# Attention's small products at new places in the projection's fill, and the mLSTM's splits ordered behind attention's exponentials

## The chip, the cores and the metric

The kernel runs on one core of one Trainium2 chip. The metric is the time on the device in microseconds (us), the median of several runs. A core has five engines that run on their own and wait for one another by semaphores: TensorE (PE in the profile; PEld is its weight load), VectorE (DVE), ScalarE (ACT), GpSimd (POOL) and SyncE (SP, which here only issues DMAs). Each engine takes its instructions in the order in which the program has them: an instruction that waits holds up all that stand behind it on its engine.

## What is computed

Two layers of a decoder trunk on 512 tokens of width 1024, in float32. Cut to what matters:

```python
h = rmsnorm(x, norm_mix)
z = h @ w_in          # attention q, k, v | mLSTM q, k, v, o-gate, i/f | branch gates A, B
att = sliding_window_attention(q_a, k_a, v_a, sinks)   # 8 heads of 64, 2 key heads, window 128
hm  = mlstm_chunkwise(q_m, k_m, v_m, i_pre, f_pre)     # 4 heads
hm  = rmsnorm(hm, head_gain) * sigmoid(o_m)
x = x + (sigmoid(g_a) * (att @ w_att_branch) + sigmoid(g_m) * (hm @ w_m_branch)) @ w_out
u = relu(rmsnorm(x, norm_ffn) @ w_ff1)
x = x + (u * u) @ w_ff2
```

Attention's queries and keys go through an RMS norm for each head and a rotation of the first 16 of 64 dimensions. Scores are masked to a band, and a learned sink for each head joins the softmax's sum.

## The kernel before

**Two stages for each layer.** `mixer` does all up to `w_out`, `mlp` the rest. The change lies in `mixer` alone, and it runs twice, once for each layer.

**Large products.** A float32 product is made of three products of halves: each operand x is split into a rounded high part (ACT, a copy to fp32r) and the rest (DVE, a subtraction). `chunk` loads 128 rows of weights and splits them so (L192 on ACT, L193 on DVE); `mm3` issues the three products (L47). The large products write "mm" tiles in PSUM, the small ones "aux" tiles. There are six "mm" banks, and only two "aux" buffers, shared by all small products.

**Fill and side.** `weave(fill, side)` sets the order in which the work is written down. The fill is a list of steps of large products, each with a width: one step is 0.25, three products of 512 columns. Four steps (one chunk of weights against four column blocks) are one unit, twelve products. The side is a list of pairs (place, function): a function is called when the fill has reached its place. Tile's planner then makes each engine's order out of it: what was written earlier has the higher rank among what the planner's own model holds to be ready, so an engine's order can depart from the lists.

**The two fills of the mixer.** The first holds attention's query projection (places 0 to 8) and its key/value projection, 264 columns wide (8 to 16). The second starts with the mLSTM's query/key projection (0 to 8), then gate groups 0 and 1 (8 to 16, 16 to 24), the mLSTM's values (24 to 32), attention's two branch products `a_steps` (32 to 40), gate group 2, the o-gate and gate group 3 (40 to 64). Beside the second fill run attention (places 0 to 23 in the lists before), the mLSTM's gating (8.45 to 17.45) and, from place 28 on, the mLSTM's decay, weights and outputs.

**Attention by units.** A unit is a block b of 128 queries and a key head kv, eight in all. Each has five steps: `att_scores` for two pairs of heads (PE; ACT copies the previous block's part, L653; DVE the masked own part, L654), `att_softmax` (DVE takes the maximum, L665 to L668; ACT the exponentials, L671 and L673; DVE the sum and the scaling, L674 to L676), `att_probs` (PE transposes, `split` on ACT and DVE, L204 and L205, masks on POOL), and `att_out` (PE against the values; ACT and DVE join and split the result, L704 to L712). Ahead of them, `k_tr` and `q_tr(b)` turn keys and queries: four transposes on PE, then pairs of ACT (L632) and DVE (L633), the next pair after the last. `q_vec` and `k_vec` scale and rotate them on DVE and POOL (the keys' last step is L598). `last_exp` holds the last exponential of the softmax that was written down last.

**The row of inverse norms.** The token norm is not applied to the input but to the projections. `norm.columns` makes it as a column for each block of tokens (L270 to L276; L276 is also the last step of the head norms' inverse roots), `norm.along` as a row: four DVE writes of a diagonal (L329), one product with ones on PE, one ACT copy (L333). The row is used by the evacuations of the mLSTM's query/key projection (L724, L726) and of the gate groups (L761).

**The mLSTM's splits.** `qk_split` makes the high and low parts of the mLSTM's queries and keys, eight calls at places 12.5 + 1.4 n: ACT copies (L732), for the queries POOL copies them and DVE subtracts (L734, L737), for the keys DVE alone subtracts (L740). Their first readers are the mLSTM's weights, from place 29.75 on.

**The sigmoids.** At place 24.5 the eight tiles of gate groups 0 and 1 go through ACT's sigmoid (L748) behind `last_exp[0]`, and `back` reloads the exponential's table behind them (L754).

An instruction inside `with tc.issue_after(i)` is put behind instruction i in the order of its engine, without a semaphore.

Of the kernel before, what the change touches and what calls it, by code (L numbers as in the profile page):

```python
# [12 lines left out]
AF = mybir.ActivationFunctionType  # L13
# [5 lines left out]
NB = T // P  # L19
# [16 lines left out]
def hybrid_kernel(ctx, tc, x, norm_mix, w_in, att_q_norm, att_k_norm, att_sinks, m_gate_bias,  # L36
# [3 lines left out]
    ve, sc, gp = nc.vector, nc.scalar, nc.gpsimd  # L40
# [299 lines left out]
    norm = norm0 = Norm(lambda k: g_mix(0, k))  # L340
# [89 lines left out]
    def mixer(l, norm, late, order, phase):  # L430
# [24 lines left out]
        row = []  # L455
# [4 lines left out]
        def ev_kv(b, ps):  # L460
# [2 lines left out]
        weave(tok_steps(acts, wcols(C_Q, 512), ev_q, order=order)  # L463
              + tok_steps(acts, lambda k: [W[k * P:(k + 1) * P, C_K:C_K + 256],
                                           W[k * P:(k + 1) * P, C_IF:C_IF + 8]], ev_kv, width=264),
              late + [(6.9, norm.columns)])


        ig = sm([P, NB, MH], "ig", 1)
# [113 lines left out]
        last_exp = []  # L583
# [31 lines left out]
        def q_vec(b):  # L615
            rope(q_tok[b].rearrange("p (h d) -> p h d", d=HD), b, HQ)

        def q_tr(b):


            ps = aux()
            for j in range(4):
                pe.transpose(ps[:, j * P:(j + 1) * P], q_tok[b][:, j * P:(j + 1) * P], ident)
            for j in range(2):
                qT[b, j] = temp(F32R)
                t4 = qT[b, j].rearrange("p (n i t) -> p n i t", n=2, i=2)
                p4 = ps[:, 2 * j * P:2 * (j + 1) * P].rearrange("p (n t) -> p n t", n=2)
                for i in range(2):
                    r = slice(64 * i, 64 * i + 64)
                    o = slice(64 - 64 * i, 128 - 64 * i)  # L630
                    g = gcols[0][r, l:l + 1]
                    sc.activation(t4[r, :, i, :], p4[r], AF.Copy, scale=g)  # L632
                    ve.scalar_tensor_tensor(t4[o, :, i, :], p4[r], g, f32(t4[r, :, i, :]), op0=ALU.mult,  # L633
                                            op1=ALU.subtract)

        def att_scores(b, kv, hp):
            if hp == 0 and b:
                sps[b, kv] = temp()
            ps = aux()
            for i in range(2):  # L640
                c = 2 * hp + i
                lhs = qT[b, kv][:, c * P:(c + 1) * P]
                o = ps[:, i * 2 * P:(i + 1) * 2 * P]
                ks = slice(b * P, (b + 2) * P)
                if b == 0:

                    o, ks = o[:, P:], slice(P, 2 * P)
                pe.matmul(o, lhs, kTh[:, kv, ks], start=True, stop=False)
                pe.matmul(o, lhs, kTl[:, kv, ks], start=False, stop=True)
            p4 = ps.rearrange("p (h w k) -> p h w k", h=2, w=2)  # L650
            dst = sps[b, kv][:, hp * 2 * P:(hp + 1) * 2 * P].rearrange("p (h k) -> p h k", h=2)
            if b:
                sc.activation(dst, p4[:, :, 0, :], AF.Copy)  # L653
            ve.copy_predicated(dst, tri_i.unsqueeze(1).to_broadcast([P, 2, P]), p4[:, :, 1, :])  # L654
# [5 lines left out]
        def att_softmax(b, kv):  # L660
            sp = sps[b, kv]
            s3 = sp.rearrange("p (h k) -> p h k", h=4)
            hs = slice(4 * kv, 4 * kv + 4)
            m = sm([P, 4], "m")
            ve.tensor_reduce(m, s3, axis=AX.X, op=ALU.max)  # L665
            ve.scalar_tensor_tensor(m, m, -1.0, nsinks[:, l, hs], op0=ALU.mult, op1=ALU.min)
            es = sm([P, 4], "es")
            ve.tensor_tensor(es, sinks[:, l, hs], m, op=ALU.add)  # L668
            den = sm([P, 4], "den")
            for i in range(4):  # L670
                sc.activation(s3[:, i, :], s3[:, i, :], AF.Exp, bias=m[:, i:i + 1],  # L671
                              accum_out=den[:, i:i + 1])
            last_exp[:] = [sc.activation(es, es, AF.Exp)]  # L673
            ve.tensor_tensor(den, den, es, op=ALU.add)  # L674
            ve.reciprocal(den, den)
            ve.tensor_tensor(s3, s3, den.unsqueeze(2).to_broadcast([P, 4, P]), op=ALU.mult)  # L676

        def att_probs(b, kv):
            sp = sps[b, kv]
            pt = aux()  # L680
            for i in range(4):
                pe.transpose(pt[:, i * P:(i + 1) * P], sp[:, i * P:(i + 1) * P], ident)
            hl = split(pt, get=lambda: temp(F32R))
            parts[b, kv] = [(hl, b)]
            if b > 0:

                prev = [temp(F32R) for _ in hl]
                for src, dst in zip(hl, prev):
                    s3, d3 = (t.rearrange("p (h q) -> p h q", h=4) for t in (src, dst))
                    gp.affine_select(out=d3, in_=s3, compare_op=ALU.is_gt, fill=0.0, base=0,  # L690
                                     pattern=[[0, 4], [-1, P]], channel_multiplier=1)
                    gp.affine_select(out=s3, in_=s3, compare_op=ALU.is_ge, fill=0.0, base=0,
                                     pattern=[[0, 4], [1, P]], channel_multiplier=-1)
                parts[b, kv].append((prev, b - 1))

        def att_out(b, kv):
            po = aux()
            ls = parts[b, kv]
            for n, (pr, kb) in enumerate(ls):
                vb = v2[:, kb, kv].rearrange("p i d -> p (i d)")  # L700
                for m, p_ in enumerate(pr):
                    pe.matmul(po, vb, p_, start=n + m == 0, stop=n == len(ls) - 1 and m == 1)
            low, both = temp(), temp()
            sc.activation(low[0:64, :], po[64:128, :], AF.Copy)  # L704
            p4, l4 = (t[0:64, :].rearrange("p (j i t) -> p j i t", j=2, i=2) for t in (po, low))
            b3 = both[:, 0:2 * P].rearrange("p (j t) -> p j t", j=2)
            for i in range(2):
                ve.tensor_tensor(b3[64 * i:64 * i + 64], p4[:, :, i, :], l4[:, :, i, :], op=ALU.add)
            for j in range(2):
                dh, dl = (a[:, b * P:(b + 1) * P] for a in att_acts[2 * kv + j])  # L710
                sc.activation(dh, b3[:, j, :], AF.Copy)
                ve.tensor_tensor(dl, b3[:, j, :], f32(dh), op=ALU.subtract)  # L712
# [15 lines left out]
        def qk_split(m, i):  # L728
            t = qk_raw[m]
            r, o = slice(64 * i, 64 * i + 64), slice(64 - 64 * i, 128 - 64 * i)  # L730
            d = slot(F32R)
            sc.activation(d[r], t[r], AF.Copy)  # L732
            if m < 2:
                gp.tensor_copy(d[o], f32(d[r]))  # L734
                low = slot(F32R)
                gp.memset(f32(low[o]), 0.0)
                ve.tensor_tensor(low[r], t[r], f32(d[r]), op=ALU.subtract)  # L737
                m_q[2 * m + i], m_ql[2 * m + i] = d, low
            else:
                ve.tensor_tensor(d[o], t[r], f32(d[r]), op=ALU.subtract)  # L740
                m_k[2 * (m - 2) + i] = d
# [27 lines left out]
        def ev_v(b, ps):  # L769
            if b == 0:  # L770
# [3 lines left out]
                          scale=norm.col[:, b:b + 1])  # L774

        units = [(b, kv) for b in range(NB) for kv in range(HKV)]
        first, apart = 5.75, 1.65
        side = [(0, lambda: q_vec(0)), (0, k_vec), (0, lambda: q_vec(1)),
                (first - 1.25, k_tr), (first - 1.75, lambda: q_tr(0))]
        for i, (b, kv) in enumerate(units):  # L780
            at = first + apart * i
            side += [(at, lambda b=b, kv=kv: att_scores(b, kv, 0)),
                     (at + 1.25, lambda b=b, kv=kv: att_scores(b, kv, 1)),
                     (at + 1.25, lambda b=b, kv=kv: att_softmax(b, kv)),
                     (at + 3.45, lambda b=b, kv=kv: att_probs(b, kv)),
                     (at + 3.45 + 2.2, lambda b=b, kv=kv: att_out(b, kv))]
            if kv == 0 and b + 1 < NB:
                if b + 2 < NB:
                    side.append((at + 1, lambda b=b: q_vec(b + 2)))
                side.append((at + 2 * apart - 1.75, lambda b=b: q_tr(b + 1)))  # L790
        side.append((1.5, lambda: row.append(norm.along())))
        side += [(8.45 + 3.0 * i, f) for i, f in enumerate((gating0, gating1, gating2, gating3))]
        side += [(12.5 + 1.4 * n, lambda n=n: qk_split(n // 2, n % 2)) for n in range(8)]
        g0, s0 = gate_steps(0)
        g1, s1 = gate_steps(1)
# [70 lines left out]
        for h in range(MH):  # L866
            at = 28 + 4.65 * h
# [32 lines left out]
        norm = Norm(lambda k: g_ffn(l, k))  # L900
# [10 lines left out]
    def mlp(l, norm, late, phase):  # L911
# [355 lines left out]
        def go(i, s, n):  # L1267
# [16 lines left out]
    late = ([(0.75 + 0.9 * (k - 2), lambda k=k: norm.turn(k)) for k in range(2, KT)]  # L1284
            + [(6.5, lambda: gains(grow, 16))]
            + [(3.0 + 2.0 * j, lambda j=j: norm.squares(j)) for j in range(2)])
# [49 lines left out]
```

## Time and profile before

| | us |
|---|---|
| median of 3 runs (1311.24 to 1312.83) | 1312.2 |
| the profiled execution | 1312.1 |
| its span, first to last instruction | 1310.4 |
| TensorE busy | 1288.5 (98%) |
| DVE busy | 961.9 (73%) |
| ACT busy | 771.2 (59%) |
| second fill, layer 0: start, reading of attention's result | 45.1, 168.98 |
| second fill, layer 1: start | 695.0 |

How to read it: the matmuls are pipelined, so one begins before the one ahead has ended, and their ends are modelled. A busy TensorE is therefore not one at full pace; the pace is read from starts, or from the chain that ended last. The view of waits says for each engine what ended its idle time; a line named there can be that of a helper (L47 is every matmul, L51 every transpose), so the tile's name beside it counts: "aux" for small products, "mm" for large ones. Granted clock is what the throttle gave TensorE, 1.00 being full speed.

### The profile page before, as it was taken

What the parts mean: (1) busy time and instruction counts of PE and PEld (TensorE: products, weight loads), DVE (VectorE), ACT (ScalarE), POOL (GpSimd) and SP (SyncE); (2) the same over time, 40 slices, a digit from 0 to 9 for tenths busy, and PEclk for the clock granted to TensorE, in tenths of its full rate; (3) what the DMA queues carried; (4) which work ended last, traced back from release to release, by engine and by line L of the source; (5) the groups of instructions that cost most, each with busy time, mean ns of one, the idle gap of its engine ahead of it and who ended that gap; (6) DMA issues with size and microseconds to landing.
All of it is one profiled execution on the core that took longest, in us unless ns stands there. A gap on an engine that the chain in (4) does not pass through costs nothing.

```text
span 1310.4 us, 19489 instructions
## 1 busy us (share of the span) xinstructions
PE 1288.5 (98%) x7126; PEld 1111.5 (85%) x7126; DVE 961.9 (73%) x1477; ACT 771.2 (59%) x1365; POOL 214.6 (16%) x303
## 2 busy tenths in 40 slices
PE   9999999999999999999999999999999999999998
PEld 7877788888899989999887777888888999999987
DVE  4689755466587897978946896645766888979786
ACT  5556755444475666667544667554444766666663
POOL 4502201100011122120014122011000111212100
PEclk9999999999999999999999999999999999999999
DMA  5322236738288999787313222367392799897743
GB/s 153 102 68 67 64 91 162 183 112 221 78 205 192 266 185 238 180 182 197 112 37 109 65 65 73 107 159 169 121 263 50 194 232 247 176 260 150 188 139 136
DMA packets 139169, 196.52 MB, mean 150 GB/s; under 512 B 10424, under 2 KB 76576, under 8 KB 139072
## 3 DMA queue, kind: packets, MB, share of 16 engines
q1 hardware_dynamic: 93040, 135.88, 33.6%
q0 software_dynamic: 37568, 44.17, 21.9%
q10 hardware_dynamic: 8464, 15.21, 3.8%
q8 instruction: 56, 0.92, 0.3%
q14 instruction: 41, 0.34, 0.1%
HBM read 193.14 MB, written 31.46 MB: 171 GB/s over the span
## 4 chain that ended last, share of the span: by engine, by line
PE 86%; DVE 6%; ACT 4%; DMA 2%; issue 2%; SPq 0%; ACTq 0%; DVEq 0%; POOLq 0%
PE mm L47 74%; PE aux L47 10%; PE aux L51 2%; DMA raw<-in_w_ff_dram 1%; ACT wh L192 1%; DVE wl L193 1%; DMA w<-in_w_in_dram 1%; ACT t L671 1%; DVE t L633 0%; DVE a L740 0%; DVE t L676 0%; ACT t L632 0%; DVE wl L942 0%; ACT wh L938 0%; DVE u L956 0%
## 5 line engine op out<-in xcount | busy, mean ns | idle before, releaser
L47 PE MATMUL mm<-i,wh 128*128 128x512 f32 (+1 forms) x1216 | 329.8, 357 | 0.0
L938 ACT ACTIVATE wh<-raw 128x1024 fp32r<-128x1024 f32 x218 | 229.4, 1056 | 136.0 <-PE mm L47 68.2
L942 DVE TENSOR_TENSOR wl<-raw,wh 128x1024 fp32r<-128x1024 f32 x218 | 264.4, 1221 | 59.7 <-ACT wh L938 58.3
L193 DVE TENSOR_TENSOR wl<-w,wh 128x512 fp32r<-128x512 f32 (+1 forms) x208 | 140.1, 675 | 128.8 <-ACT wh L192 121.0
L47 PEld LDWEIGHTS mm<-i,wh 128*128 128x128 f32 x1216 | 210.5, 190 | 25.9 <-issue 0.5
L192 ACT ACTIVATE wh<-w 128x512 fp32r<-128x512 f32 (+1 forms) x208 | 127.0, 612 | 149.0 <-PE mm L47 122.9
L47 PE MATMUL mm<-i,wl 128*128 128x512 f32 (+1 forms) x608 | 214.3, 352 | 0.0
L47 PE MATMUL mm<-wh,uh 128*128 128x512 f32 x448 | 175.0, 391 | 0.0
L47 PE MATMUL mm<-wl,uh 128*128 128x512 f32 x448 | 174.7, 390 | 0.0
L47 PE MATMUL mm<-wh,ul 128*128 128x512 f32 x448 | 174.3, 389 | 0.0
L982 POOL DMA_DIRECT2D raw<-in_w_ff_dram x56 | 72.7, 1298 | 496.2 <-DVE wl L942 326.5
L47 PE MATMUL mm<-wh,i 128*128 128x512 f32 (+1 forms) x512 | 149.2, 368 | 1.0 <-ACT wh L192 0.7
L47 PEld LDWEIGHTS mm<-i,wl 128*128 128x128 f32 x608 | 115.4, 190 | 15.4 <-issue 0.5
L47 PE MATMUL mm<-hs,wh 128*128 128x256 f32 x672 | 122.2, 283 | 0.7 <-ACT u L1173 0.7
L47 PEld LDWEIGHTS mm<-hs,wh 128*128 128x128 f32 x672 | 105.7, 192 | 2.2 <-ACT u L1173 1.1
L47 PEld LDWEIGHTS mm<-wh,i 128*128 128x128 f32 x512 | 91.7, 188 | 17.1 <-DVE i L208 1.1
L47 PEld LDWEIGHTS mm<-wh,ul 128*128 128x128 f32 x448 | 84.1, 188 | 17.8
L47 PEld LDWEIGHTS mm<-wh,uh 128*128 128x128 f32 x448 | 84.3, 188 | 16.5
L47 PEld LDWEIGHTS mm<-wl,uh 128*128 128x128 f32 x448 | 84.2, 188 | 16.0
L47 PE MATMUL mm<-hs,wl 128*128 128x256 f32 x336 | 95.1, 283 | 0.0
L47 PE MATMUL mm<-wl,i 128*128 128x512 f32 (+1 forms) x256 | 93.1, 364 | 0.0
L996 DVE SCALAR_TENSOR_TENSOR x<-mm,ninv,x 128x512 f32<-128x512 f32 x112 | 81.0, 745 | 10.2 <-PE mm L47 10.0
(245 smaller groups left out, 2164.5 us busy)
## 6 DMA issues: line engine op xcount, KB each, us to landing
raw<-in_w_ff_dram SPq DMA_DIRECT2D x124, 512.0 KB, 5.9
w<-in_w_in_dram SPq DMA_DIRECT2D x128, 256.0 KB, 2.7
raw<-in_w_ff_dram POOLq DMA_DIRECT2D x56, 512.0 KB, 7.7
sum<-in_w_ff_dram ACTq DMA_DIRECT2D x28, 512.0 KB, 5.3
raw<-sum SPq DMA_DIRECT2D x28, 512.0 KB, 4.3
sum<-in_w_ff_dram POOLq DMA_DIRECT2D x20, 512.0 KB, 6.3
w<-in_w_out_dram SPq DMA_DIRECT2D x32, 256.0 KB, 3.3
w<-in_w_att_branch_dram SPq DMA_DIRECT2D x16, 256.0 KB, 2.6
```

The costliest lines, as they stand in the source:

```text
L47: return nc.tensor.matmul(*args, **kw)
L51: return nc.tensor.transpose(*args)
L192: last_wh[:] = sc.activation(wh[:, :off], raw[:, :off], AF.Copy), wh
L193: ve.tensor_tensor(wl[:, :off], raw[:, :off], f32(wh[:, :off]), op=ALU.subtract)
L671: sc.activation(s3[:, i, :], s3[:, i, :], AF.Exp, bias=m[:, i:i + 1], accum_out=den[:, i:i + 1])
L938: last_wh[:] = sc.activation(hi, r, AF.Copy), hi[:, 0, :]
L942: ve.tensor_tensor(lo, r, f32(hi), op=ALU.subtract)
L982: nc.gpsimd.dma_start(r, w1_block(k, n, c0), accum_op=ALU.add)
L996: ve.scalar_tensor_tensor(xh[:, i, :], ps[i], norm.inv[:, 0 if sign > 0 else 1, b:b + 1], xh[:, i, :], op0=ALU.mult, op1=ALU.add)
```

## The change

Three edits, all in `mixer`. `norm.along` is called at place 12.0 of the first fill instead of 1.5 of the second. `qk_split`'s ACT copy is put behind the last exponential that has been written down by then. The regular spacing of attention's steps (5.75 + 1.65 for each unit, the steps at fixed distances) and of the gating steps (3.0 apart) is replaced by tables of places.

```diff
-              late + [(6.9, norm.columns)])
+              late + [(6.9, norm.columns), (12.0, lambda: row.append(norm.along()))])
...
             d = slot(F32R)
-            sc.activation(d[r], t[r], AF.Copy)
+            with tc.issue_after(last_exp[0].ins):
+                sc.activation(d[r], t[r], AF.Copy)
...
-        first, apart = 5.75, 1.65
-        side = [(0, lambda: q_vec(0)), (0, k_vec), (0, lambda: q_vec(1)),
-                (first - 1.25, k_tr), (first - 1.75, lambda: q_tr(0))]
-        for i, (b, kv) in enumerate(units):
-            at = first + apart * i
-            side += [(at, lambda b=b, kv=kv: att_scores(b, kv, 0)),
-                     (at + 1.25, lambda b=b, kv=kv: att_scores(b, kv, 1)),
-                     (at + 1.25, lambda b=b, kv=kv: att_softmax(b, kv)),
-                     (at + 3.45, lambda b=b, kv=kv: att_probs(b, kv)),
-                     (at + 3.45 + 2.2, lambda b=b, kv=kv: att_out(b, kv))]
-            if kv == 0 and b + 1 < NB:
-                if b + 2 < NB:
-                    side.append((at + 1, lambda b=b: q_vec(b + 2)))
-                side.append((at + 2 * apart - 1.75, lambda b=b: q_tr(b + 1)))
-        side.append((1.5, lambda: row.append(norm.along())))
-        side += [(8.45 + 3.0 * i, f) for i, f in enumerate((gating0, gating1, gating2, gating3))]
+        at = ((6.01, 7.2, 11.24, 15.13),
+              (7.7, 8.96, 14.87, 16.06),
+              (10.42, 12.3, 16.06, 22.38),
+              (12.78, 15.73, 21.77, 24.28),
+              (15.73, 16.59, 23.76, 26.45),
+              (18.95, 23.45, 25.47, 27.04),
+              (23.65, 24.31, 27.02, 30.18),
+              (25.45, 26.45, 30.03, 31.05))
+        turn_at = (4.0, 7.7, 12.55, 18.93)
+        gate_at = (8.45, 15.31, 21.98, 26.19)
+        side = [(0, lambda: q_vec(0)), (0, k_vec), (0, lambda: q_vec(1)), (4.5, k_tr)]
+        side += [(turn_at[b], lambda b=b: q_tr(b)) for b in range(NB)]
+        for (b, kv), (s0_, s1_, p_, o_) in zip(units, at):
+            side += [(s0_, lambda b=b, kv=kv: att_scores(b, kv, 0)),
+                     (s1_, lambda b=b, kv=kv: att_scores(b, kv, 1)),
+                     (s1_, lambda b=b, kv=kv: att_softmax(b, kv)),
+                     (p_, lambda b=b, kv=kv: att_probs(b, kv)),
+                     (o_, lambda b=b, kv=kv: att_out(b, kv))]
+            if kv == 0 and b + 2 < NB:
+                side.append((s0_ + 1, lambda b=b: q_vec(b + 2)))
+        side += list(zip(gate_at, (gating0, gating1, gating2, gating3)))
```

In each row of the table stand the places of a unit's two score steps (the softmax goes with the second), its probabilities and its output. `turn_at` is for `q_tr`, `gate_at` for the gating steps. No instruction's work is changed.

## The prediction

> **What bounds the kernel now.** I read the page first, then TensorE's waits over the whole run, then the order of time around the longest waits, then the busy time of each engine by stretch.
>
> ```profile
> span 1310.4 us, 19489 instructions
> PE 1288.5 (98%) x7126; PEld 1111.5 (85%) x7126; DVE 961.9 (73%) x1477; ACT 771.2 (59%) x1365; POOL 214.6 (16%) x303
> ...
> L193 DVE TENSOR_TENSOR wl<-w,wh 128x512 fp32r<-128x512 f32 (+1 forms) x208 | 140.1, 675 | 128.8 <-ACT wh L192 121.0
> ```
>
> TensorE is busy 98% of the span (the last row, DVE's half of a weight split with its mean of 675 ns, is for later), so time can come only out of its own pauses or out of slowly running products. This change removes no product. What it can win is bounded by the pauses in the stretch that it touches, once in each of the two layers. TensorE's waits (who waited, for whom, us in total, times, longest), the rows of that stretch:
>
> ```profile
> PE aux L47 <- ACT t L632: 4.9, 2, 2.4
> PE aux L51 <- DVE t L654: 3.1, 4, 1.3
> PE aux L47 <- DVE rqk L276: 2.8, 2, 1.5
> PE aux L47 <- DVE t L708: 1.7, 4, 0.6
> PE aux L51 <- DVE t L676: 0.8, 2, 0.4
> PE aux L47 <- DVE t L633: 0.6, 2, 0.3
> PE aux L51 <- DVE es L668: 0.4, 2, 0.2
> PE aux L51 <- ACT wh L192: 0.4, 1, 0.4
> PE aux L51 <- DVE t L708: 0.2, 1, 0.2
> ```
>
> Together 14.9 us in 20 waits, all before small products ("aux"), none before the large ones ("mm"). A wait costs more than its idle time. In order of time, around the longest one in layer 0 and the same one in layer 1:
>
> ```profile
> 76.69 0.40 PE L47 MATMUL mm<-i,wl 128*128 128x512 f32 x1
> 79.51 0.79 PE L47 MATMUL aux<-kT,t 128*128 128x256 f32 x4 [2.43 <-ACT t L632]
> ...
> 729.27 0.71 PE L47 MATMUL aux<-kT,t 128*128 128x256 f32 x4 [2.43 <-ACT t L632]
> ...
> 52.93 5.72 PE mm L47 x25
> 79.51:83.48 3.97, 3.97 (x15) 3.32 (x15) 3.61 (x8) 0.54 (x2) 0.00 (x0) 0.57 0.25 68
> 729.27:732.00 2.73, 2.73 (x15) 2.12 (x16) 2.60 (x5) 0.55 (x2) 0.00 (x0) 1.00 0.15 24
> ```
>
> The third row from the end is from the chain that ended last: 25 large products in 5.72 us, 0.23 us from one to the next, though each shows 0.40 (they overlap). So a wait costs its idle time and about 0.40 - 0.23 = 0.17 us of lost overlap; 20 waits make 3.4 us. The last two rows are stretches; the number behind POOL's count is the granted clock. After 2.43 us of waiting, layer 0 ran 3.97 us at a clock of 0.57, layer 1 at 1.00. Layer 0 lost 3.97 x 0.43 = 1.7 us that way. **The ceiling is 14.9 + 3.4 + 1.7 = 20.0 us.**
>
> The Trainium skill, "TensorE: Matmul & The Clock Gate", Part 1, says that the clock halves after about 3.4 us without work, counted in a free-running window, and returns after as long at work. Here 2.43 us was enough once and not the other time, so the length stated is not a threshold in this trace. By that rule no shorter wait would cost clock and the 1.7 us would not recur.
>
> **The change part by part.**
>
> *The places.* The large products form a fill: twelve of them (four steps of 0.25) are one unit of the lists. The number of "mm" products between the fill's start and a small product gives its place now. The rows count them from 45.21 us; two of the count are the tail of the product before.
>
> ```profile
> 45.21:79.50 34.29, 27.73 (x113) 1.00 0.32 86
> 45.21:117.75 72.54, 58.27 (x231) 0.98 0.28 74
> 45.21:153.10 107.89, 82.28 (x325) 0.98 0.27 72
> ```
>
> Scores of block 1: (113 - 2)/12 = 9.25, new place 10.42. Probabilities of the fourth unit: 229/12 = 19.08, new 21.77. The last output: 323/12 = 26.92, new 31.05. The shift grows to 4.1 units, 4.1 x 12 x 0.23 = 11.3 us. The waits with their overlap and the slow clock, without that for L276, come to (14.9 - 2.8)/2 + 9 x 0.17 + 1.7 = 9.3 us in layer 0. So the new places put each small product at about the clock time at which it runs now, with large products where TensorE waits, and some 2 us to spare at the end. The order among the small products barely changes. That takes out the waits if the chain behind them (scores, maximum, exponentials, probabilities on ACT and DVE) keeps its present times.
>
> *The row of inverse norms* (norm.along) moves from 1.5 in this fill to 12.0 in the one before.
>
> ```profile
> 29.49 0.16 DVE L276 TENSOR_TENSOR ncol<-ncol,nru 128x4 f32<-128x4 f32 x1
> 51.84 1.10 PE L47 MATMUL aux<-t,ones 128*128 128x512 f32 x2 [1.47 <-DVE rqk L276]
> ```
>
> Its product costs 1.10 us in either place. What goes is the wait, 2.8 us in both layers and 0.3 of overlap. Its column is ready at 29.65, long before 12.0, and its four DVE writes then stand in a queue that holds weight splits only, not the head norms' chain (L276) that they now run among. The wait there is between 0 and the present 1.5 us; I take 0.3 us a layer, half a weight split that may be in front. Its early end also brings everything behind it forward by 1.6 us. The tightest of the first links, the keys' rotation before their transposition, allows it:
>
> ```profile
> 57.37 0.87 POOL L598 TENSOR_TENSOR kvi<-rp,rq 128x128 f32<-128x128 f32 x1
> 60.55 0.60 PE L51 MATMUL aux<-ident,kvi 128*128 128x128 f32 x4
> ```
>
> The keys are ready at 58.24, 2.3 us ahead of their product.
>
> *The splits for the mLSTM* get an order behind the latest exponentials at their place in the list: three behind those of the third unit, five behind the fifth's.
>
> ```profile
> 75.52 1.28 ACT L732 ACTIVATE a<-a 64x512 fp32r<-64x512 f32 x2
> 77.20 0.62 ACT L732 ACTIVATE a<-a 64x512 fp32r<-64x512 f32 x1
> 107.49 2.57 ACT L732 ACTIVATE a<-a 64x512 fp32r<-64x512 f32 x4
> 115.05 0.19 ACT L673 ACTIVATE es<-es 128x4 f32<-128x4 f32 x1
> L740 DVE TENSOR_TENSOR a<-a,a x8: 684/686/690, 113.7 to 768.7; 64x512 fp32r<-64x512 f32 x8
> ```
>
> Three of them now stand at 75.5 to 77.8 among the ACT steps L632 that the 2.43 us wait is for: 3 x 0.62 = 1.9 us leave that chain, a margin just where the longest wait was. The same work returns later: five on ACT (3.1 us) after 115.05 instead of from 107.5, with 5 x 0.69 = 3.4 us on DVE. Queued behind them are the evacuations of scores and turned queries. DVE's room (stretch, its length, then busy time of PE, PEld, DVE, ACT, POOL):
>
> ```profile
> 70.00:110.00 40.00, 37.35 (x191) 30.42 (x191) 34.16 (x85) 25.78 (x74) 6.40 (x10) 0.96 0.24 62
> 110.00:150.00 40.00, 36.89 (x179) 28.27 (x178) 36.05 (x82) 26.27 (x78) 11.47 (x17) 1.00 0.23 64
> 150.00:170.00 20.00, 20.00 (x90) 16.47 (x90) 9.64 (x23) 17.24 (x38) 3.59 (x7) 1.00 0.27 80
> ```
>
> Without its waits there the fill advances some 1.5 units further from 110 to 150. Each unit brings 0.7 us of weight split (L193) and 0.3 of evacuation (a gate group's four of 0.62 in eight units): 1.5 us. One more split's DVE part falls into the stretch, 0.7; the other four stand there already. So 36.05 becomes some 38.3 of 40 us: hardly room. I expect the chain to slip there, by nothing at the least and at the most by all waits of the second half, 4.2 us a layer (of the waits' rows, halved: 1.3 for L654, 0.95 for L708, 0.4 for L676, 0.2 each for L668 and L192, and seven times 0.17). The 2 us to spare cover half: I take 2.0 us a layer.
>
> *The sigmoids* of the first two gate groups are not edited, but they go behind the latest exponentials traced at 24.5: now the eighth unit's, afterwards the seventh's (24.31; the eighth's stand at 26.45).
>
> ```profile
> 136.57 0.19 ACT L673 ACTIVATE es<-es 128x4 f32<-128x4 f32 x1
> 144.96 0.40 ACT L671 ACTIVATE t<-t,m 128x128 f32<-128x128 f32 x1 [1.30 <-DVE m L666]
> L748 ACT ACTIVATE a<-a x32: 615/619/634, 149.2 to 922.6; 128x512 f32<-128x512 f32 x32
> L748 ACT ACT_TABLE_LOAD  x4: 1283/1283/1283, 147.9 to 872.0; - x4
> 142.39 1.87 DVE L761 TENSOR_TENSOR a<-mm,t 128x512 f32<-128x512 f32 x3
> 158.58 0.49 DVE L712 TENSOR_TENSOR u<-t,u 128x128 fp32r<-128x128 f32 x2
> 168.98 0.62 PE L47 MATMUL mm<-u,wh 128*128 128x512 f32 x2
> ```
>
> Eight sigmoids (5.0), a table load on each side (2.6) and two weight splits (taken as long as DVE's, 1.3) are 8.9 us; ACT has 144.96 - 136.76 = 8.2 us between the two units. Their input, the second gate group's evacuation (L761), comes some 10 us earlier than 142.4 with the fill. So the eighth unit is late by 0 to 1 us; I take 0.5 a layer. Attention must also end in time for the product that reads it. Its last write ends at 159.07, that product starts at 168.98, afterwards at some 158; but it begins with the first key group, and needs the eighth unit two places later, 2 x 12 x 0.23 = 5.5 us, at some 163. So 4 us are left.
>
> The Trainium skill, "ScalarE: Activation LUTs", What ACT_TABLE_LOAD costs, gives 1.28 us for a load and 1.38 for the drain with it. The trace agrees on the load (1283 ns) and shows no drain: the first load starts at 147.9, the first sigmoid at 149.2. By the page's figure, as an estimate, the eighth unit would be later by 2 x 1.38 = 2.8 us a layer and the sum worse by up to 5.5; I go by the rows.
>
> **Sum.** 20.0 us less 2 x (0.3 + 2.0 + 0.5) = 5.6 leaves 14.4 us. The profiled execution took 1312.1 us (1310.4 of span, 1.7 around it), 0.1 below the median of 1312.2: 1312.1 - 14.4 = 1297.7. **I predict 1298 us.**
>
> **The rivals.**
> *DVE is the bound and returns most of it.* With 38.3 of 40 us filled, all late waits come back in both layers (8.4), and half of the L632 ones (5.2 with overlap, half is 2.6): 20.0 - 8.4 - 2.6 - 1.6 = 7.4, 1304.7. For it: DVE's rows. Against: from 150 on it has half its time free and the new places reach there.
> *The change doesn't do what it says:* a place in the list gives only rank, and the planner issues what it thinks ready. The splits listed from 12.5 on ran at 75.5, place 9. If small products get ahead likewise, only the row's wait goes, 2.5 us: 1309.6. Against: none of the small products counted above stands ahead of its present listed place (9.25 against 9.05, 19.08 against 14.15, 26.92 against 22.95).
> *Slower: the sigmoids hold the eighth unit.* If they come only when its maximum is ready (145), it slips 8.9 us; TensorE waits in order before its probabilities, and a wait that long also loses clock, 1.7: 10.6 a layer, 21.2 in all. 1298 + 21 = 1319. It decides from a slip of 7.2 us a layer (half of 14.4), 8.5 to be measurable. Against: the seventh unit's exponentials end at 136.8 and the input is earlier.
>
> **How the numbers follow.** A run of this kernel can tell about 0.2%, 2.6 us, from no change. Forecast (1292 to 1302) 0.58; DVE as bound (1302 to 1309) 0.22; better than the ceiling 0.03, since an earlier ACT could also free small losses that I didn't count; not as it says (1309 to 1314) 0.09; slower 0.08. The range from 1291.5 to 1308 leaves out 0.2. Faster 0.83, same 0.09, slower 0.08.
>
> **What would show it.** Right: the L632 wait and the L276 wait gone in both layers; TensorE's idle from the fill's start to the branch product under 3 us a layer; no stretch at a clock below 0.9; L732 behind the third and fifth unit's exponentials; sigmoids ahead of the eighth unit's. DVE as bound: its share from 110 to 150 above 95%, with waits on L654, L676 and L708 still there. Sigmoids: a wait of several us before the last unit's probabilities. Wrong altogether, if the waits go and the time stays: then the later stages gave it back, which now show hardly a pause, or weights came late ("mm" waiting for L192 or a DMA).

## The result

The changed kernel is slower: 1321.5 us median (1320.2 to 1321.8) against 1311.9 for the kernel before on the same chip. One more of its runs took 2143 us at a granted clock of 0.56; one run of the kernel before was slow in the same way (1579 us at 0.75), and the figures here leave such runs out. The ratio is 1.0071, 95% interval 1.0056 to 1.0086. The prediction was 1298 us with a range up to 1308, so it is wrong in sign. The profiled execution took 1321.5 us.

The page of the changed kernel, its span and its engines (busy us, share of the span):

```profile
span 1319.8 us, 19489 instructions
...
PE 1294.2 (98%) x7126; PEld 1116.2 (85%) x7126; DVE 962.1 (73%) x1477; ACT 769.0 (58%) x1365; POOL 219.2 (17%) x303
```

The number of instructions is the same, and so is the work. TensorE's waits after (who waited, for whom, us in total, times, longest):

```profile
PE aux L47 <- ACT t L812: 6.9, 2, 3.4
PE aux L47 <- DVE t L708: 4.1, 6, 1.1
PE aux L51 <- DVE t L654: 3.6, 4, 1.0
PE aux L47 <- DVE t L831: 2.0, 2, 1.5
```

The waits for L632 (4.9) and L276 (2.8) are gone, as forecast. The waits for L654 and L708 are not: both are longer than before (3.1 and 1.7). In the place of the first two stand waits of other lines: L812, an ACT copy of the mLSTM's decay row, and L831, the last step of a weighting there, neither of which stood among the waits of the kernel before. Where they stand is seen in order of time, end of the fill of layer 0 (start, length, instruction, the idle time before it):

```profile
145.46 0.64 PE L47 MATMUL aux<-kT,t 128*128 128x256 f32 x4
...
155.96 0.60 PE L51 MATMUL aux<-ident,t 128*128 128x128 f32 x4
...
164.32 0.74 PE L47 MATMUL aux<-a,a 128*128 128x512 f32 x2 [3.45 <-ACT t L812]
...
167.17 2.07 PE L47 MATMUL aux<-t,v 128*128 128x512 f32 x4 [1.47 <-DVE t L831]
...
170.96 2.04 PE L47 MATMUL aux<-t,v 128*128 128x512 f32 x4 [1.08 <-DVE t L708]
172.80 1.05 PE L47 MATMUL mm<-u,wh 128*128 128x512 f32 x2
```

The row at 170.96 is attention's last output, that at 172.80 the branch product that reads attention (168.98 before). Between them TensorE only does what is left of attention, with pauses and at a low clock. Stretches of the same trace (length, busy time of PE, PEld, DVE, ACT, POOL, then granted clock):

```profile
110.00:150.00 40.00, 37.75 (x183) 29.50 (x182) 32.95 (x71) 26.63 (x70) 12.83 (x19) 1.00 0.23 65
...
163.68:175.50 11.82, 8.63 (x24) 6.24 (x25) 7.08 (x19) 6.42 (x19) 3.17 (x7) 0.60 0.05 20
```

Comparing the starts of the same large products in both traces says where the time went. The first large product behind the second gate group, at place 24 (143.06 before), starts at 129.21, 13.8 us earlier. This is a lead, and most of it is not work saved: 104 small products with 16.0 us of TensorE's time stand ahead of that point in this fill, where 154 with 25.9 us stood before; the others now come behind it. At the branch product all of the lead is gone and 3.8 us more. Layer 1 repeats it: 8.8 us ahead of before at 782.9, 8.6 behind at 826.3. **The large products ran ahead and attention did not follow; at place 32 they waited for it.** The runs below ask what held attention.

### The profile page after: what moved, and what is told of

Its sections match the earlier page's. It is cut to its first block, busy times and chain, and to the rows that moved or that the text cites. A ratio compares the mean times of both kernels' runs of the same rounds, so it can differ in the third digit from the quotient of the medians.

```text
span 1319.8 us, 19489 instructions
## 1 busy us (share of the span) xinstructions
PE 1294.2 (98%) x7126; PEld 1116.2 (85%) x7126; DVE 962.1 (73%) x1477; ACT 769.0 (58%) x1365; POOL 219.2 (17%) x303
## 4 chain that ended last, share of the span: by engine, by line
PE 89%; DVE 5%; ACT 3%; DMA 1%; issue 1%; POOL 1%; SPq 0%; ACTq 0%; DVEq 0%; POOLq 0%
PE mm L47 77%; PE aux L47 10%; PE aux L51 2%; DMA w<-in_w_in_dram 1%; DVE wl L193 1%; ACT t L671 1%; ACT wh L192 1%; DVE t L708 0%; DVE a L741 0%; DVE a L762 0%; DVE t L654 0%; DVE t L633 0%; ACT t L704 0%; DVE t L676 0%; DVE t L525 0%
## 5 line engine op out<-in xcount | busy, mean ns | idle before, releaser
L47 PE MATMUL mm<-i,wh 128*128 128x512 f32 (+1 forms) x1216 | 325.7, 355 | 0.0
L47 PEld LDWEIGHTS mm<-i,wl 128*128 128x128 f32 x608 | 115.1, 189 | 15.4
```

The costliest lines, as they stand in the source:

```text
L47: return nc.tensor.matmul(*args, **kw)
```

## The experiments

All times are medians; each ratio is to the kernel before on the same chip. The suspects are the tie of the splits (their `issue_after`) and the sigmoids, which by their place 24.5 now pass the last two units of attention.

**Sigmoids behind attention's last exponentials.** In the changed kernel:

```diff
-        side.append((24.5, lambda: back(sigmoid(g0 + g1, last_exp[0]))))
+        side.append((26.5, lambda: back(sigmoid(g0 + g1, last_exp[0]))))
```

> The changed kernel with one number different: the sigmoids of gate groups 0 and 1 at place 26.5 instead of 24.5, so that they go behind the eighth unit's exponentials as they did before the change. Theory S (the sigmoids between the seventh and the eighth unit's exponentials hold attention's end, 8.2 us on ACT in each layer): TensorE's 3.4 us wait for L812 and the waits behind it shrink, the branch product of layer 0 starts near 165 instead of 172.8, and the time falls by some 16 us to 1306. Theory B (the chain is late before that, from the turned queries of block 2 on, because DVE takes the fill's evacuations and the splits first): the eighth unit's probabilities stay at fill 32, the sigmoids now delay the mLSTM's exponentials instead, and the time stays within 4 us of 1321.6.

1320.1 us, ratio 1.0067 (1.0047 to 1.0086): nothing won. ACT in that run:

```profile
151.15 1.28 ACT L749 ACT_TABLE_LOAD   x1
...
161.18 1.28 ACT L755 ACT_TABLE_LOAD   x1
162.48 0.59 ACT L704 ACTIVATE t<-aux 64x512 f32<-64x512 f32 x1
163.09 0.60 ACT L812 ACTIVATE t<-aux 128x512 f32<-128x512 f32 x1
```

The block still stands in the chain: behind it now wait the copy of the sixth unit's output (L704, its product ran at 147.40) and the decay row (L812). These hold both small banks, and no other small product can start for 13 us. Place 26.5 was not late enough.

**No tie.** The two lines of `issue_after` in `qk_split` undone, everything else as changed.

```diff
-            with tc.issue_after(last_exp[0].ins):
-                sc.activation(d[r], t[r], AF.Copy)
+            sc.activation(d[r], t[r], AF.Copy)
```

> The changed kernel without the tie: the mLSTM's splits on ACT are free again to run when ACT has room. Theory B: three splits leave DVE between 91 and 96 us and five between 118 and 126, the lag of 5.4 us at the first unit's output falls to some 3 and that at the sixth unit's second scores (8.3) to some 5, the branch product starts 3 to 4 us earlier, time 1313 to 1316. Theory S alone: the lag before the sigmoids does not matter, time within 2 us of 1321.6. The tie helps, as the prediction had it: the wait at block 1's scores comes back, 1324 or more.

1308.0 us, ratio 0.9974 (0.9964 to 0.9984). Faster than before, and by more than any of the three expectations gave: the tie costs 13.6 us here. But this is far from 1298. The second suspect is seen in it, on ACT:

```profile
137.34 1.28 ACT L748 ACT_TABLE_LOAD   x1
...
144.24 1.28 ACT L754 ACT_TABLE_LOAD   x1
...
146.29 0.60 ACT L704 ACTIVATE t<-aux 64x512 f32<-64x512 f32 x1
146.91 0.38 ACT L653 ACTIVATE t<-aux 128x256 f32<-128x256 f32 x1
```

and on TensorE, the seventh unit's probabilities, its output and the branch product:

```profile
147.97 0.60 PE L51 MATMUL aux<-ident,t 128*128 128x128 f32 x4
...
159.53 1.34 PE L47 MATMUL aux<-t,v 128*128 128x512 f32 x4 [2.67 <-DVE t L830]
...
164.43 1.05 PE L47 MATMUL mm<-u,wh 128*128 128x512 f32 x2
```

At the eighth unit's scores (137.70) this chain is where it was before (137.47). Then the sigmoids hold ACT for 8.2 us, and the seventh unit's probabilities come 8.5 us later than before (139.50).

**The row alone.** The kernel before with the first hunk of the change and nothing else:

```diff
-              late + [(6.9, norm.columns)])
+              late + [(6.9, norm.columns), (12.0, lambda: row.append(norm.along()))])
...
-        side.append((1.5, lambda: row.append(norm.along())))
```

> The kernel before with the first edit alone: the row of inverse norms in the fill before. Every theory: the wait for L276 goes, 1.6 us in each layer. If attention's chain follows, 1309 (the prediction's term: 2.5 us). If the chain is bound by DVE and ACT and not by TensorE, the same us come back as waits before scores and probabilities, 1311 to 1312.

1309.4 us, ratio 0.9986 (0.9977 to 0.9996): 0.14%, 1.8 us of the 2.5 forecast, and the wait for L276 is gone.

**Row and tie at the old places.** As the last, with the tie:

```diff
-            sc.activation(d[r], t[r], AF.Copy)
+            with tc.issue_after(last_exp[0].ins):
+                sc.activation(d[r], t[r], AF.Copy)
```

> The kernel before with the row's new place and the tie, attention's and the gating's places as before. Theory S or B (the loss comes from the new places, which let the fill's evacuations and sigmoids get ahead of attention): no loss here, the wait of 2.43 us before block 1's scores shrinks by 1.5 or more in each layer, 1303 to 1309. If the tie itself is what costs (DVE's backlog behind the third and fifth unit's exponentials), 1312 to 1318.

1318.3 us, ratio 1.0057 (1.0041 to 1.0073). The tie costs 8.9 us without any new place. Its trace has a hole in the large products that the run without the tie doesn't have. First with the tie:

```profile
111.89 0.40 PE L47 MATMUL mm<-i,wl 128*128 128x512 f32 x1
...
120.96 2.47 DVE L762 TENSOR_TENSOR a<-mm,t 128x512 f32<-128x512 f32 x4
...
121.89 0.63 PE L47 MATMUL mm<-i,wh 128*128 128x512 f32 x2
```

then the same evacuation of the first gate group without it:

```profile
104.17 2.47 DVE L761 TENSOR_TENSOR a<-mm,t 128x512 f32<-128x512 f32 x4
```

The evacuation stands 16.8 us later. The large products have three pairs of banks (`which = "xyf"[turn_of[0] % 3]`), and a group takes two of them. The second gate group's second pair is one that the first group holds until L762. In the order of instructions of this kernel, 24 matmuls of the second group go to its first pair, then come only small products, then L762, then the rest. In DVE's order L762 stands just ahead of the third split's DVE half. The next run tests that link.

**The third split free.** As the last, with

```diff
-            with tc.issue_after(last_exp[0].ins):
+            with ExitStack() as own:
+                if (m, i) != (1, 0):
+                    own.enter_context(tc.issue_after(last_exp[0].ins))
```

> As e4_old_places (old places, row early, tie: 1318.3, against 1309.4 without the tie), with the tie taken from the third of the eight splits alone. In e4_old_places the evacuation of the first gate group stands in DVE's queue just ahead of that split's DVE part, at 120.96 us in place of 104.17; until then the second gate group can run in one of its two pairs of banks only, and the large products stop from 112 to 122. Theory (the tie costs by that evacuation): evacuation at 103 to 107, no stop at 112 to 122, 1309 to 1312. Rival (the tied splits cost by where they stand in ACT's and DVE's queues; seven of eight still do): 1315 to 1319.

1307.1 us, ratio 0.9964 (0.9953 to 0.9975), better than expected, and the evacuation is back:

```profile
108.07 2.47 DVE L764 TENSOR_TENSOR a<-mm,t 128x512 f32<-128x512 f32 x4
```

At the old places the tie's cost hangs on one split of eight. The other seven gain 0.22% over the row alone; the wait for L632 is 2.4 us in both layers there, in place of 4.9.

**Sigmoids behind all of attention, no tie.** The changed kernel without the tie, and

```diff
-        side.append((24.5, lambda: back(sigmoid(g0 + g1, last_exp[0]))))
+        side.append((31.2, lambda: back(sigmoid(g0 + g1, last_exp[0]))))
```

> The new places without the tie, as in e2_no_tie (1308.0), with the sigmoids of the first two gate groups listed at 31.2 (behind all of attention) in place of 24.5. In e2_no_tie the eighth unit's scores start at 137.7 us, as in the kernel before (137.5), but eight sigmoids with their table load hold ACT from 137.3 to 145.5, and the seventh unit's probabilities come at 148.0 (139.5 before). Theory (the block of sigmoids gives the places' gain back at the branch product): the seventh unit's probabilities at 139 to 142, attention's last output before 160, branch product at 158 to 162 in place of 164.4, so 3 to 6 us a layer less: 1296 to 1303. Rival (attention can't end earlier with the large products run ahead of it, whoever stands on ACT; the sigmoids only stand in time that is lost anyway): branch product at 163 to 166, 1306 to 1310. A third outcome, above 1310: the sigmoids now stand in front of the mLSTM's exponentials (and switch tables among them) and that costs as much.

1297.5 us, ratio 0.9897 (0.9882 to 0.9912): the best of all kernels here, and 10.5 us below the same kernel with 24.5 (0.77%, or 10.1 us, by the ratios; the two ran on different chips). The seventh unit's probabilities, attention's last output and the branch product:

```profile
141.04 0.60 PE L51 MATMUL aux<-ident,t 128*128 128x128 f32 x4
...
158.53 1.16 PE L47 MATMUL aux<-t,v 128*128 128x512 f32 x4
159.99 0.62 PE L47 MATMUL mm<-u,wh 128*128 128x512 f32 x2
```

Its stretch, and all that is left of TensorE's waits in the second fills:

```profile
110.00:150.00 40.00, 39.93 (x200) 32.79 (x199) 34.82 (x83) 27.00 (x79) 13.73 (x20) 1.00 0.23 67
```

```profile
PE aux L47 <- DVE t L830: 2.0, 5, 0.8
...
PE aux L47 <- DVE t L654: 0.7, 2, 0.3
PE aux L51 <- DVE m L666: 0.4, 2, 0.2
```

The sigmoids now mix with the mLSTM's exponentials on ACT and change its table six times for it where two were enough, 1.28 us each; with waits this small nothing on TensorE shows for it.

**The control: sigmoids at 31.2 with the old places.** The run with the row alone, and the same line of the sigmoids at 31.2.

> As e3_row_only (old places, row early, no tie: 1309.4), with the sigmoids listed at 31.2 as in e5_sig_end (1297.5). It differs from e5_sig_end by the table of places alone. Theory (the places are the gain; the sigmoids only take it away when they pass the last units): at the old places they rank behind attention with 24.5 too, so nothing changes, 1307 to 1311. Rival (a good part of the 11.8 us between e3_row_only and e5_sig_end is the sigmoids' later place): 1300 to 1306.

1308.5 us, ratio 0.9983 (0.9973 to 0.9992), as the row alone. So it is the places that win, 0.86% of the 1.03%, and the sigmoids' rank only decides whether the win is kept.

**Half way.** The changed kernel without the tie, each place of attention's table the mean of old and new, sigmoids at 28.5; `turn_at` and `gate_at` stay as changed (shown are the first and the last row of the table):

```diff
-        at = ((6.01, 7.2, 11.24, 15.13),
+        at = ((5.88, 7.1, 10.22, 13.27),
...
-              (25.45, 26.45, 30.03, 31.05))
+              (21.38, 22.5, 25.39, 27.0))
```

> No tie; every place of attention half way between its old and its new one; sigmoids listed at 28.5, which is behind the eighth unit's probabilities. Theory (sigmoids out of the chain, and attention's end at a place that it can hold): the waits mostly gone up to fill 24, branch product at 157 to 161 us, 1294 to 1301. Rival (the end of attention is fixed by its own chain): 1304 to 1310.

1303.4 us, ratio 0.9941 (0.9926 to 0.9956), above what the theory gave and just below the rival. Part of the old waits is there again, so these places were not late enough:

```profile
PE aux L47 <- ACT t L632: 3.4, 2, 1.7
PE aux L47 <- DVE t L708: 2.4, 2, 1.2
```

**The tie at the new places, with the sigmoids out of the way.** The changed kernel with the sigmoids at 31.2, all eight splits tied; then the first three alone, as below, and the last five alone, with `m > 1 or (m, i) == (1, 1)` as the condition.

```diff
-            with tc.issue_after(last_exp[0].ins):
+            with ExitStack() as own:
+                if m == 0 or (m, i) == (1, 0):
+                    own.enter_context(tc.issue_after(last_exp[0].ins))
```

> The changed kernel with its tie and its places, sigmoids listed at 31.2. Against e5_sig_end it differs by the tie alone. Theory (the tie slips the attention chain by itself, 5 us at the first unit's output and 8 by the fourth's, and these slips are not made good): 8 to 14 us slower than e5_sig_end, 1306 to 1316. Rival (the tie costs only where the slipped chain meets the sigmoids): within 3 us of e5_sig_end.

> As e5_sig_end (1297.5, no tie, sigmoids behind all of attention), with the tie on the first three splits only. With all eight tied (e8_tie_sig_end) it took 1315.3; there the first unit's output is 5 us later (99.8 us against 94.6), and from the fourth unit on the chain is 6 us later, attention's last output 8 us (166.5 against 158.5). Theory (a slip of the chain is made good as long as ACT and DVE have room behind it; it stays when the later tied splits stand behind it too): the first unit's output again at 99 to 101, but the sixth unit's second scores back at 124 to 126, 1297 to 1302. Rival (the first slip carries through the chain to the branch product whatever follows): 1303 to 1310.

> As e5_sig_end, with the tie on the last five splits only. Theory (as for e9_tie_first3): no slip at the first unit's output (94 to 96 us), little later, 1295 to 1301. Rival (the later five splits are the cost by themselves, since they stand ahead of evacuations from 119 to 125 us): the sixth unit's second scores at 129 to 132, 1306 to 1313.

All eight: 1315.3, ratio 1.0030 (1.0018 to 1.0041). The first three: 1301.2, 0.9926 (0.9909 to 0.9943). The last five: 1298.4, 0.9903 (0.9889 to 0.9918). Against no tie that is +1.33%, +0.29% and +0.06%, of which the last can't be told from nothing: the costs don't add. The first unit's output and attention's last one, all eight tied:

```profile
99.84 0.62 PE L47 MATMUL aux<-t,v 128*128 128x512 f32 x2
...
166.50 1.66 PE L47 MATMUL aux<-t,v 128*128 128x512 f32 x4 [3.23 <-DVE t L708]
```

the first three:

```profile
99.76 0.63 PE L47 MATMUL aux<-t,v 128*128 128x512 f32 x2
...
159.91 1.16 PE L47 MATMUL aux<-t,v 128*128 128x512 f32 x4
```

the last five:

```profile
94.45 0.63 PE L47 MATMUL aux<-t,v 128*128 128x512 f32 x2
...
159.19 1.17 PE L47 MATMUL aux<-t,v 128*128 128x512 f32 x4
```

The first three make the first slip of 5 us by themselves, and alone it is made good down to 1.4 us at the last output (158.53 without a tie). With the later five tied behind it, the slip stays and grows to 8.0.

How the three splits make the first slip is read in the changed kernel, on ACT and DVE in order of time:

```profile
90.08 0.62 ACT L733 ACTIVATE a<-a 64x512 fp32r<-64x512 f32 x1
90.73 0.47 ACT L632 ACTIVATE t<-aux,gc 64x256 fp32r<-64x256 f32 x1
91.10 0.61 ACT L733 ACTIVATE a<-a 64x512 fp32r<-64x512 f32 x1
...
92.28 0.62 ACT L733 ACTIVATE a<-a 64x512 fp32r<-64x512 f32 x1
92.92 0.47 ACT L632 ACTIVATE t<-aux,gc 64x256 fp32r<-64x256 f32 x1
...
95.17 0.68 DVE L738 TENSOR_TENSOR a<-a,a 64x512 fp32r<-64x512 f32 x1
...
96.38 2.71 DVE L762 TENSOR_TENSOR a<-mm,t 128x512 f32<-128x512 f32 x4
...
99.72 0.49 DVE L633 SCALAR_TENSOR_TENSOR t<-aux,gc,t 64x256 fp32r<-64x256 f32 x1
```

L632 and L633 turn the third block's queries. They hold a small bank until the last of them, at 99.72, and the three splits (L733, with L738 on DVE) and the gate group's evacuation stand among them. The first unit's output, 95.11 before, starts at 100.47. With the sigmoids at 31.2 and no tie, the last L633 goes ahead of the evacuation, which stands at nearly the same time:

```profile
93.30 0.49 DVE L633 SCALAR_TENSOR_TENSOR t<-aux,gc,t 64x256 fp32r<-64x256 f32 x1
...
95.49 1.28 DVE L761 TENSOR_TENSOR a<-mm,t 128x512 f32<-128x512 f32 x2
```

With the tie DVE has hardly any room from 90 to 100 us. The stretch in the changed kernel, then in the run without a tie (the third busy time is DVE's; it is 7.73 in the kernel before):

```profile
90.00:100.00 10.00, 9.02 (x42) 7.23 (x41) 9.53 (x17) 5.92 (x13) 3.81 (x5) 1.00 0.28 79
90.00:100.00 10.00, 10.00 (x56) 8.26 (x55) 8.89 (x18) 5.97 (x12) 0.61 (x1) 1.00 0.30 82
```

## Why the prediction was wrong, by its own steps

In per cent of the time before, the runs divide the change thus: places, row and sigmoids kept behind attention -1.03; the sigmoids passing two units +0.77 (0.9974 less 0.9897); the tie +0.97 (1.0071 less 0.9974). The sum is +0.71. The division goes by one order of the steps: with the sigmoids at 31.2 the tie costs 1.33, and 24.5 in place of 31.2 then adds only 0.41 (1.0071 less 1.0030). The two partly spend the same time.

*The ceiling and the places: right.* I wrote that "the new places put each small product at about the clock time at which it runs now, with large products where TensorE waits". Without the harm of the tie and the sigmoids that is what is seen: 39.93 us of products in the 40 from 110 to 150, at a clock of 1.00, and the eighth unit's scores at 138.49 for 137.47. On the way the chain is later by up to 5.2 us (the third unit's probabilities, 105.17 for 99.94) and makes it good. Of the ceiling of 20.0 us, 3.1 us of waits in nine places are left in the second fills, with 0.17 each 4.6; 15.4 were to be won and 13.5 (by the ratio) to 14.4 (by the medians) were. That this is also the 14.4 of the sum is chance: the sum had taken off 5.0 for a chain slip and sigmoids that the best kernel doesn't have.

*The row: right in mechanism,* 1.8 us for 2.5.

*The tie: the step that failed.* I wrote that three splits "leave that chain, a margin just where the longest wait was". That part happened: the wait for L632 went. But a tied split isn't gone; it comes back at a place that the tie chooses, and there stand the third block's L632 and L633 steps. I had named what is "queued behind them" and then priced it by DVE's busy time from 110 to 150 and by the waits of the kernel before, "at the most by all waits of the second half, 4.2 us a layer". Both were the wrong measure. The slip begins 20 us earlier: from 90 to 100 DVE is busy 9.53 of 10 us, while from 110 to 150, where I forecast 38.3 of 40, it is busy 32.95. (The best kernel has 34.82 there, with 200 matmuls in place of 179.) And what the slip costs is not the old waits but the large products' lead: they had to wait for attention ahead of the branch product, in waits of lines (L812, L831) that the old rows don't hold, with a clock of 0.60 behind them. The tie took 0.97%, 6.4 us a layer, where 2.0 were taken and 4.2 allowed.

*The sigmoids: sized at 0.5 us a layer, measured at 5.0* (0.77% is 10.1 us in two layers). I set 8.9 us of sigmoids into a gap of "144.96 - 136.76 = 8.2 us between the two units". The gap was not free. The kernel before has in it:

```profile
137.73 0.60 ACT L704 ACTIVATE t<-aux 64x512 f32<-64x512 f32 x1 [0.85 <-PE aux L47]
138.35 0.38 ACT L653 ACTIVATE t<-aux 128x256 f32<-128x256 f32 x1
```

These two copies, 1 us of ACT, empty both small banks, and one of them brings the eighth unit's scores whose maximum the exponentials of 144.96 wait for. Behind the sigmoids they come at 146.29 and 146.91. I had taken the eighth unit's input as given and asked only whether its exponentials were late.

*The rivals.* The slower one, 1319, came close in time by luck and names half the cause: the sigmoids hold both last units by the banks, not the eighth by its maximum, and without the tie they leave the kernel still faster than before. "DVE is the bound" fits the 10 us from 90 to 100 and the waits on L654 and L708, which stayed; as the bound from 110 to 150 it falls by DVE's 32.95 of 40 us, and by the best kernel's 39.93 us of products beside 34.82 of DVE. "The change doesn't do what it says" falls with the waits that went.

*What stays open.* Why the first gate group's evacuation is put behind the third split when that is tied is not to be seen in a trace: the order of instructions is fixed before the run; shown is that it hangs on this split. Which of the last five turns the made-good slip into one that stays was not divided further.

## What to carry to other kernels

Before large work is let run ahead of a dependent chain, find the place where it must wait for that chain's end, and price every edit by what it does to that end: here a lead of 13.8 us was gone at one product. An instruction that is tied to another isn't taken off the path; look at what the queue holds at its new place, and above all whether something there frees a shared buffer, since a copy of 0.4 us can hold a bank for 9 (in the run without the tie, the scores of 137.70 were copied at 146.91). An engine's busy time has to be taken over the stretch in which the chain passes it: here 10 us told what 40 hid. An engine that shows a gap between two steps of a chain may have the chain's own short links in it.

## What the hardware showed that I had not expected

In the changed kernel the granted clock is 0.60 over 11.8 us after the wait of 3.45 us. The same wait in layer 1 is followed by 0.50 over 8.3 us. The run without the tie shows it after waits of 2.67 and 1.08 us (its stretch, then length, busy times and clock):

```profile
162.59:167.00 4.41, 4.41 (x12) 3.55 (x13) 2.82 (x9) 2.37 (x8) 0.29 (x1) 0.50 0.00 0
```

TensorE is busy for all of the 4.41 us and still gets half the clock. The Trainium skill, "TensorE: Matmul & The Clock Gate", Part 1, has the clock halve after about 3.4 us without work. The 3.45 us agree; 2.67 followed by 1.08 do not reach it one by one, nor do 2.12 followed by 1.11 in the run with row and tie at the old places (0.54 over the next 3.45 us), and 2.43 in the kernel before was enough in one layer and not in the other. What the slow clock costs, as an estimate, is the busy time times the part of the clock that is missing: 8.63 x 0.40 = 3.5 us after the 3.45, and 4.41 x 0.50 = 2.2 us in the stretch above. For pricing, these traces say that a wait of some 2 us or more may cost nearly as much again in clock, and that its length alone doesn't decide.
